# Score matmuls issued in turn for the two halves of the rows, and the norms' reciprocal roots as a power on GpSimd

## The chip, the cores and the metric

The kernel runs on one core of a Trainium2 chip. The core has a matmul engine (TensorE, PE in the profile, with its weight loads shown as PEld), VectorE (DVE), ScalarE (ACT), GpSimd (POOL) and a queue that issues transfers (SyncE, SP). The metric is device time in microseconds from the first to the last instruction of one execution; lower is better.

## The reference, cut to what matters

256 rows of width 1024 go through two layers of a first block and two layers of a second block, all in float32. What bears on the change:

```python
def rms_norm(x, g):
    y = x * lax.rsqrt(jnp.mean(x * x, axis=-1, keepdims=True) + EPS)
    return y * g

# first block, for each 128-row half t of the rows, 16 heads of 64:
logits = einsum("bqhd,bsd->bqhs", iqb, ik)            # 8 index heads of 64
score  = einsum("bqh,bqhs->bqs", iwb, relu(logits)) * IDX_SCALE
# the 64 best keys of each row are kept; the rest is masked
s = einsum("bqhd,bqkhd->bhqk", qb, kg) * scale
p = softmax(where(valid, s, -inf))
# second block: 8 heads of 96 the same way without selection, and a gated
# linear attention over chunks of 64:
a_intra = where(causal, einsum('bhncd,bhnsd->bhncs', q_t, k_t), 0.0)
```

Every `rms_norm` needs one reciprocal root for each row and normed group: of the whole row (ahead of each projection), of each head (q and k), of each of four groups of the state-space output, and of the latent vectors of the second block.

## The kernel before, in words

The work is one long program of projections. Activations lie transposed (features on partitions), 256 rows wide. Each weight slab of 128 by 1024 floats is loaded by SyncE into `raw` (line 443), copied to a high part by ScalarE (`whi`, line 446), and the rest is made by VectorE (`wlo`, line 447); 639 such slabs stream through five `raw` buffers. `lin_t` (lines 482 to 484) and `add_n` (499 to 501) then make three reduced-precision matmuls in place of each full one. Matmuls between activations (scores, transposes, sums) are made in float32, and each of them shows as two matmul instructions in the trace.

PSUM has four `pmm` tiles for projections and four `px` tiles for all else: scores, transposes (672), the sums of squares of a norm (554), the spreading of its root (575), and the modulation columns (`ada_part`, 697 to 702).

The order on each engine is not the written one. Every instruction has a priority by its place in the program (weight loads and splits have a raised one), and a planner that simulates the timeline picks, for each engine, the ready instruction of the best priority. Each engine then works its list strictly in order. Side work (attention, the linear attention, preparations) is written as Python generators that the projection loops advance step by step, so that its instructions fall between projections.

`rsqrt(v, n)` (lines 534 to 544) makes the root of n columns: a shifted bit pattern as first guess (538, 539) and three Newton steps of three operations (541 to 543), eleven VectorE instructions in a chain. It is called 28 times: 8 times by `Norm.close` for whole rows (n = 2), 8 times by `ssm_norm` (n = 2), 4 times for the heads of the first block (n = 32), 4 times for those of the second (n = 16), twice for the latents (n = 4) and twice in `gla` (n = 8). The value `v` comes from `mean_eps` (548). For n = 2 two matmuls against the identity (575) turn the root into a row that is copied (632) or used from PSUM.

Score matmuls of 64 features read rows 0 to 63 or rows 64 to 127 of the array, by the parity of the head. Before, `attention` issues for each 128-row half t two tiles: heads h0 and h0+2 (one parity), then h0+1 and h0+3 (the other), with a yield of the generator between them. `index_scores` issues for e = 0 and then e = 1 a tile of two heads each, and `gla` writes tile q = 0 and then q = 1 of a pair j.

Of the kernel before, what the change touches and what calls it, by code (L numbers as in the profile page):

```python
# [19 lines left out]
F32 = mybir.dt.float32  # L20
F32R = mybir.dt.float32r
I32 = mybir.dt.int32
AF = mybir.ActivationFunctionType
OP = mybir.AluOpType
AX = mybir.AxisListType

EPS = 1e-6
RSQRT_BITS = 0x5F3759DF
T = 256
D = 1024  # L30
NEG = -3.0e38
# [302 lines left out]
def program(ctx: ExitStack, tc: tile.TileContext, a, out, pp_at, cst_at):  # L334
    nc = tc.nc
    V, S, G, PE, SY = nc.vector, nc.scalar, nc.gpsimd, nc.tensor, nc.sync

    cpool = ctx.enter_context(tc.tile_pool(name="cpool", bufs=1))
# [43 lines left out]
        S.dma_start(pp[0], a["pp"][:, :PP0])  # L382
    V.memset(ones, 1.0)
    V.memset(eps, EPS)
    V.memset(hpi, math.pi / 2)

    def C(key):
        o, n = cst_at[key]
        return cst[1][:, o - 128:o - 128 + n] if o else cst[0]
# [18 lines left out]
    def t512(name="t512", dt=F32):  # L408
        return tmp.tile([128, 512], dt, name=name, tag="t512", bufs=N512)
# [4 lines left out]
    def tiny(n, name="tiny"):  # L414
        return tmp.tile([128, n], F32, name=name, tag=f"tiny{n}", bufs={24: 1, 16: 4, 64: 1}.get(n, 8))

    def pmm():
        return ps_mm.tile([128, 512], F32, name="pmm", tag="pmm", bufs=4)

    def px():  # L420
        return ps_x.tile([128, 512], F32, name="px", tag="px", bufs=4)
# [96 lines left out]
    def new_hl(n, name):  # L518
        k = (n + 3) // 4
        return HL([slot(F32R, name + "h") for _ in range(k)], [slot(F32R, name + "l") for _ in range(k)])  # L520

    def to_hl(dst, k, src, bias=None, scale=None, eng=None):

        if bias is not None:
            S.activation(dst.hi(k), src, AF.Identity, bias=bias)
            V.scalar_tensor_tensor(dst.lo(k), src, bias, dst.hi(k), OP.add, OP.subtract)  # L526
        elif scale is not None:
            S.activation(dst.hi(k), src, AF.Copy, scale=scale)
            V.scalar_tensor_tensor(dst.lo(k), src, scale, dst.hi(k), OP.mult, OP.subtract)
        else:  # L530
            S.activation(dst.hi(k), src, AF.Copy)
            (eng or V).tensor_tensor(dst.lo(k), src, dst.hi(k), OP.subtract)  # L532

    def rsqrt(v, n):

        q, r = tiny(n, "rq"), tiny(n, "rr")
        ri = r.bitcast(I32)
        V.tensor_scalar(ri, v.bitcast(I32), 1, None, OP.logical_shift_right)
        V.tensor_scalar(ri, ri, -1, RSQRT_BITS, OP.mult, OP.add)
        for _ in range(3):  # L540
            V.tensor_tensor(q, r, r, OP.mult)
            V.scalar_tensor_tensor(q, q, -0.5, v, OP.mult, OP.mult)
            V.scalar_tensor_tensor(r, q, 1.5, r, OP.add, OP.mult)
        return r

    def mean_eps(ss, n, width, eps_=EPS):
        v = tiny(n, "rv")
        V.tensor_scalar(v, ss, 1.0 / width, eps_, OP.mult, OP.add)
        return v
# [221 lines left out]
    def attention(heads, qT, kT, scale, bias, vN, out_hl):  # L771

        for h0 in heads:
            pr = {}
            for t, hs in ((1, (h0, h0 + 2)), (1, (h0 + 1, h0 + 3)), (0, (h0, h0 + 2)), (0, (h0 + 1, h0 + 3))):
                nk, nh = 128 * (t + 1), 2
                ps = px()[:, :2 * nk]
                for j, h in enumerate(hs):
                    PE.matmul(ps[:, j * nk:(j + 1) * nk], qT(h)[:, t * 128:(t + 1) * 128], kT(h)[:, :nk],  # L779
                              start=True, stop=True)  # L780
                s = t512("sc") if t else tmp.tile([128, 256], F32, name="sc", tag="sc", bufs=NSC)
                s = s.rearrange("p (h k) -> p h k", h=nh)
                V.scalar_tensor_tensor(s, ps.rearrange("p (h k) -> p h k", h=nh), scale,
                                       bias(t)[:, None, :].to_broadcast([128, nh, nk]), OP.mult, OP.add)
                m = tiny(4, "m")
                V.tensor_reduce(m[:, :nh], s, AX.X, OP.max, negate=True)
                z = tiny(4, "z")
                for j in range(nh):
                    S.activation(s[:, j, :], s[:, j, :], AF.Exp, bias=m[:, j:j + 1], accum_out=z[:, j:j + 1])
                V.reciprocal(z[:, :nh], z[:, :nh])  # L790
                for j, h in enumerate(hs):
                    V.tensor_scalar(s[:, j, :], s[:, j, :], z[:, j:j + 1], 0.0, OP.mult, OP.add)
                    pr[h, t] = s[:, j, :]
                yield
            for hp in range(h0, h0 + 4, 2):
                pt = {}
                for h in (hp, hp + 1):
                    ps = px()
                    PE.transpose(ps[:, 0:128], pr[h, 0], ident)
                    PE.transpose(ps[:, 128:256], pr[h, 1][:, 0:128], ident)  # L800
                    PE.transpose(ps[:, 256:384], pr[h, 1][:, 128:256], ident)
                    pt[h] = t512("pt")
                    S.activation(pt[h][:, :384], ps[:, :384], AF.Copy)
                po = px()
                for h in (hp, hp + 1):
                    e = (h % 2) * 64
                    PE.matmul(po[e:e + 64, :256], vN(0, h), pt[h][:, :256],  # L807
                              start=True, stop=False, skip_group_check=True)
                for h in (hp, hp + 1):
                    e = (h % 2) * 64  # L810
                    PE.matmul(po[e:e + 64, 128:256], vN(1, h), pt[h][:, 256:384],
                              start=False, stop=True, skip_group_check=True)
                to_hl(out_hl, hp // 2, po[:, :256])
                yield
# [8 lines left out]
    def block1(l):  # L823
# [6 lines left out]
        h = new_hl(8, "h")  # L830
# [19 lines left out]
        ps, pn = px(), [[pmm(), pmm()] for _ in range(2)]  # L850
# [49 lines left out]
        def index_scores(t, iqT, ikT):  # L900
            nk = 128 * (t + 1)
            iws = tiny(8, "iws")
            V.tensor_scalar(iws, mN[:, t, 96:104], IDX_SCALE, None, OP.mult)
            cz = C("caus")[:, 256 - nk:]
            sc = tmp.tile([128, nk], F32, name="bias", tag=f"bias{t}", bufs=1)
            for j in range(0, 4, 2):
                for e in range(2):
                    pl = px()
                    for i in range(2):
                        PE.matmul(pl[:, i * nk:(i + 1) * nk], iqT[64 * e:64 * e + 64, j + i, t * 128:(t + 1) * 128],  # L910
                                  ikT[64 * e:64 * e + 64, :nk], start=True, stop=True)
                    rl = t512("rl")
                    S.activation(rl[:, :2 * nk], pl[:, :2 * nk], AF.Relu)
                    for i in range(2):
                        V.scalar_tensor_tensor(sc, rl[:, i * nk:(i + 1) * nk],
                                               iws[:, 2 * (j + i) + e:2 * (j + i) + e + 1],
                                               cz if j + e + i == 0 else sc, OP.mult, OP.add)
            yield
            for r in range(8):
                m8 = tiny(8, "m8")  # L920
                V.max(m8, sc)
                V.match_replace(sc, m8, sc, SENT)
            V.tensor_scalar(sc, sc, SPLIT_AT, NEG, OP.is_gt, OP.mult)
            V.tensor_tensor(sc, sc, cz, OP.min)
            bias[t] = sc
# [46 lines left out]
        qT = lambda hh: TT["q"][hh // 8][64 * (hh % 2):64 * (hh % 2) + 64, (hh // 2) % 4, :]  # L972
        kT = lambda hh: TT["k"][hh // 8][64 * (hh % 2):64 * (hh % 2) + 64, (hh // 2) % 4, :]
# [29 lines left out]
        for g in range(4):  # L1003
            bc = {}
            for i, nm in enumerate("bc"):
                ps = lin_t("w_in", h, range(8))
# [20 lines left out]
        for n in range(16):  # L1027
            for _ in range(24 * (n + LAG) // 16 - 24 * (n + LAG - 1) // 16 if n + LAG else 0):
                next(att, None)
            g, j = divmod(n, 4)  # L1030
            if j == 0:
                ys[g] = slot(name="xs")
            ps = lin_t("w_in", h, range(8))
# [106 lines left out]
        for j in range(8):  # L1140
            ps = lin_t("w_out", mx, range(8))
# [38 lines left out]
        for j in range(8):  # L1180
            ps = lin_t("w_down", f, range(22))
# [490 lines left out]
    def gla(l, ef, gqf, gkf, ke, gvN, gr, ob):  # L1672
# [5 lines left out]
                         [ke[:, j * 256 + t * 128:j * 256 + (t + 1) * 128] for j in range(2)], 128, 128)  # L1678
        pms = [px(), px()]
        for j in range(2):  # L1680
            for q in range(2):
                for t in range(2):
                    c0 = j * 256 + t * 128
                    PE.matmul(pms[q][:, c0:c0 + 128], gkf[64 * q:64 * q + 64, c0:c0 + 128],
                              gqf[64 * q:64 * q + 64, c0:c0 + 128], start=True, stop=True)
# [6 lines left out]
        for n in range(3):  # L1692
            for hh in range(4):
                j, q = hh // 2, hh % 2
# [7 lines left out]
        for hh in range(4):  # L1702
            j, q = hh // 2, hh % 2
# [11 lines left out]
        pss, oos = px(), []  # L1715
# [19 lines left out]
        r = rsqrt(mean_eps(pss[:, :8], 8, 128), 8)  # L1735
# [43 lines left out]
```

## Time and profile before

| | us |
|---|---|
| median of 3 runs | 2309.45 |
| all runs | 2316.24, 2309.45, 2309.44 |
| profiled execution | 2316.91 |
| its span in the trace | 2315.1 |

The profiled execution is one more run with the profiler on; its span is the time from its first to its last instruction, and 1.8 us lie around it. It stands with the slowest of the three runs. Times in the rows are microseconds from the start of the span. A matmul's end is modelled in the trace, so a run of matmuls is best timed from its first start to the start of what follows.

### The profile page before, as it was taken

To read this page: it belongs to the slowest core of one execution; us is meant where nothing else is said; L and a number is where in the kernel's file an instruction comes from. 1 tells how busy PE (TensorE), PEld (TensorE's weight loads), DVE (VectorE), ACT (ScalarE), POOL (GpSimd) and SP (SyncE) were. 2 spreads that over 40 slices of the span, in tenths; PEclk is the share of its full clock that TensorE was granted. 3 is DMA by queue.
4 is the path that set the end of the run, shared out by engine and by line. 5 is a ranking of instruction groups with operands and counts; after the bars stand their busy time and mean duration, and the time that the engine had idled before them with its cause. 6 is when DMAs were issued, how large, how long until landed. Compare 5 with 4: busy or idle time off the path is not lost.

```text
span 2315.1 us, 46342 instructions
## 1 busy us (share of the span) xinstructions
PE 2214.8 (96%) x18142; PEld 2077.9 (90%) x18142; DVE 1745.4 (75%) x3612; ACT 1319.7 (57%) x2462; POOL 64.8 (3%) x94
## 2 busy tenths in 40 slices
PE   7999899999999999899989999989999999899999
PEld 5888798898998878888989998889999998899999
DVE  4688778669877689878689786867785578678853
ACT  4555666457656555665467655656565455555643
POOL 0000001000000000012000000000000000000000
PEclk9999999999999999999999998999999999999999
DMA  8665344665676664344655574734555546345553
GB/s 296 214 228 199 132 146 156 225 213 193 220 241 216 221 219 155 126 152 154 225 170 189 177 247 155 229 124 151 179 178 183 184 165 217 116 150 180 184 184 125
DMA packets 143466, 429.22 MB, mean 185 GB/s; under 512 B 34864, under 2 KB 40976, under 8 KB 143248
## 3 DMA queue, kind: packets, MB, share of 16 engines
q1 hardware_dynamic: 136496, 422.24, 55.4%
q10 hardware_dynamic: 6752, 4.02, 0.5%
q8 instruction: 143, 2.34, 0.4%
q14 instruction: 75, 0.61, 0.1%
HBM read 413.98 MB, written 12.22 MB: 184 GB/s over the span
## 4 chain that ended last, share of the span: by engine, by line
PE 88%; DVE 7%; DMA 3%; ACT 2%; issue 1%; SPq 0%; ACTq 0%; DVEq 0%
PE pmm L482 22%; PE pmm L483 22%; PE pmm L484 22%; PE pmm L499 3%; PE pmm L500 3%; PE pmm L501 3%; PE px L697 2%; DVE wlo L447 2%; DMA raw<-in_w 1%; PE px L779 1%; PE px L807 1%; PE px L1103 1%; ACT whi L446 1%; PE px L672 1%; DMA raw<-in_ada 1%
## 5 line engine op out<-in xcount | busy, mean ns | idle before, releaser
L446 ACT ACTIVATE whi<-raw 128x1024 fp32r<-128x1024 f32 x639 | 674.8, 1059 | 615.4 <-PE pmm L483 402.8
L447 DVE TENSOR_TENSOR wlo<-raw,whi 128x1024 fp32r<-128x1024 f32 x639 | 783.3, 1227 | 318.6 <-PE pmm L484 218.8
L482 PE MATMUL pmm<-hh,whi 128*128 128x256 f32 x2464 | 712.0, 290 | 38.2 <-DVE xs L980 11.4
L484 PE MATMUL pmm<-hh,wlo 128*128 128x256 f32 x2464 | 708.9, 289 | 2.4 <-DVE wlo L447 2.4
L483 PE MATMUL pmm<-hl,whi 128*128 128x256 f32 x2464 | 710.2, 289 | 0.7 <-DVE hl L526 0.4
L482 PEld LDWEIGHTS pmm<-hh,whi 128*128 128x128 f32 x2464 | 482.4, 196 | 47.1 <-issue 11.3
L484 PEld LDWEIGHTS pmm<-hh,wlo 128*128 128x128 f32 x2464 | 482.1, 196 | 6.2 <-issue 2.9
L483 PEld LDWEIGHTS pmm<-hl,whi 128*128 128x128 f32 x2464 | 482.7, 196 | 4.8 <-issue 2.1
L482 PE MATMUL pmm<-fh,whi 128*128 128x256 f32 x864 | 244.9, 284 | 0.0
L483 PE MATMUL pmm<-fl,whi 128*128 128x256 f32 x864 | 244.5, 283 | 0.0
L484 PE MATMUL pmm<-fh,wlo 128*128 128x256 f32 x864 | 244.3, 284 | 0.0
L482 PEld LDWEIGHTS pmm<-fh,whi 128*128 128x128 f32 x864 | 165.7, 192 | 0.5
L483 PEld LDWEIGHTS pmm<-fl,whi 128*128 128x128 f32 x864 | 165.7, 192 | 0.2
L484 PEld LDWEIGHTS pmm<-fh,wlo 128*128 128x128 f32 x864 | 165.5, 192 | 0.5 <-issue 0.2
L500 PE MATMUL pmm<-wlo,hh 128*128 128x512 f32 x256 | 103.5, 404 | 0.0
L499 PE MATMUL pmm<-whi,hh 128*128 128x512 f32 x256 | 100.7, 406 | 0.0
L501 PE MATMUL pmm<-whi,hl 128*128 128x512 f32 x256 | 100.3, 400 | 0.0
L483 PE MATMUL pmm<-yl,whi 128*128 128x256 f32 x256 | 73.0, 288 | 1.1 <-DVE yl L532 1.0
L484 PE MATMUL pmm<-yh,wlo 128*128 128x256 f32 x256 | 72.2, 287 | 0.3 <-DVE wlo L447 0.3
L482 PE MATMUL pmm<-yh,whi 128*128 128x256 f32 x256 | 72.1, 286 | 0.0
L697 PE MATMUL px<-raw,cwide 128*32 128x128 f32 x1536 | 66.5, 287 | 4.3 <-DMA raw<-in_ada 4.0
L697 PEld LDWEIGHTS px<-raw,cwide 128*32 128x32 f32 x1536 | 41.8, 112 | 19.3 <-issue 11.1
(553 smaller groups left out, 4247.6 us busy)
## 6 DMA issues: line engine op xcount, KB each, us to landing
raw<-in_w SPq DMA_DIRECT2D x639, 512.0 KB, 3.7
raw<-in_ada SPq DMA_DIRECT2D x96, 512.0 KB, 4.3
csb<-csd SPq DMA_DIRECT2D x16, 512.0 KB, 5.8
phd<-phases SPq DMA_DIRECT2D x8, 512.0 KB, 3.6
phasel<-phd SPq DMA_DIRECT2D x8, 512.0 KB, 4.4
dpd<-dp SPq DMA_DIRECT2D x4, 512.0 KB, 3.5
gl<-gd SPq DMA_DIRECT2D x32, 64.0 KB, 3.5
bl<-in_s5b SPq DMA_DIRECT2D x4, 512.0 KB, 5.5
```

The lines of the kernel that those rows point to most:

```text
L446: S.activation(hi, raw, AF.Copy)
L447: V.tensor_tensor(lo, raw, hi, OP.subtract)
L482: PE.matmul(ps[:m, :n], wh, src.hi(kt), start=q == 0, stop=False)
L483: PE.matmul(ps[:m, :n], wh, src.lo(kt), start=False, stop=False)
L484: PE.matmul(ps[:m, :n], wl, src.hi(kt), start=False, stop=q == len(kts) - 1)
L499: PE.matmul(ps[t][:, :n], src.hi(kt)[:, ts], w[0], start=start, stop=False)
L500: PE.matmul(ps[t][:, :n], src.hi(kt)[:, ts], w[1], start=False, stop=False)
L501: PE.matmul(ps[t][:, :n], src.lo(kt)[:, ts], w[0], start=False, stop=stop)
L672: PE.transpose(ps[:m, j * ncol:(j + 1) * ncol], s, ident[:ncol, :ncol])
L697: PE.matmul(pa[32 * j:32 * j + 32, :128], cwide[:, i, :], w[:, i * 128:(i + 1) * 128], start=i < 4, stop=i >= 4, skip_group_check=True)
L779: PE.matmul(ps[:, j * nk:(j + 1) * nk], qT(h)[:, t * 128:(t + 1) * 128], kT(h)[:, :nk], start=True, stop=True)
L807: PE.matmul(po[e:e + 64, :256], vN(0, h), pt[h][:, :256], start=True, stop=False, skip_group_check=True)
```

## The change

The eleven instructions of `rsqrt` become one: GpSimd raises `v` to the power of a column that holds -0.5. The column is set once at the start by VectorE. The score matmuls are issued head by head in turn for the two parities, into two PSUM tiles that are taken together; in `attention` this moves the second tile's matmuls ahead of the first tile's softmax and of the yield behind it. Nothing else is changed.

```diff
+    mhalf = cpool.tile([128, 1], F32, name="mhalf")
+    V.memset(mhalf, -0.5)
...
     def rsqrt(v, n):
-        q, r = tiny(n, "rq"), tiny(n, "rr")
-        ri = r.bitcast(I32)
-        V.tensor_scalar(ri, v.bitcast(I32), 1, None, OP.logical_shift_right)
-        V.tensor_scalar(ri, ri, -1, RSQRT_BITS, OP.mult, OP.add)
-        for _ in range(3):
-            V.tensor_tensor(q, r, r, OP.mult)
-            V.scalar_tensor_tensor(q, q, -0.5, v, OP.mult, OP.mult)
-            V.scalar_tensor_tensor(r, q, 1.5, r, OP.add, OP.mult)
+        r = tiny(n, "rr")
+        G.tensor_tensor(r, v, mhalf.to_broadcast([128, n]), OP.pow)
         return r
...
             for t, hs in ((1, (h0, h0 + 2)), (1, (h0 + 1, h0 + 3)), (0, (h0, h0 + 2)), (0, (h0 + 1, h0 + 3))):
                 nk, nh = 128 * (t + 1), 2
-                ps = px()[:, :2 * nk]
-                for j, h in enumerate(hs):
-                    PE.matmul(ps[:, j * nk:(j + 1) * nk], qT(h)[:, t * 128:(t + 1) * 128], kT(h)[:, :nk],
-                              start=True, stop=True)
+
+                if hs[0] == h0:
+                    pss = [px()[:, :2 * nk] for _ in range(2)]
+                    for h in range(h0, h0 + 4):
+                        j = (h - h0) // 2
+                        PE.matmul(pss[(h - h0) % 2][:, j * nk:(j + 1) * nk], qT(h)[:, t * 128:(t + 1) * 128],
+                                  kT(h)[:, :nk], start=True, stop=True)
+                ps = pss[hs[0] - h0]
...
             for j in range(0, 4, 2):
+                pls = [px(), px()]
+                for i in range(2):
+                    for e in range(2):
+                        PE.matmul(pls[e][:, i * nk:(i + 1) * nk],
+                                  iqT[64 * e:64 * e + 64, j + i, t * 128:(t + 1) * 128],
+                                  ikT[64 * e:64 * e + 64, :nk], start=True, stop=True)
                 for e in range(2):
-                    pl = px()
-                    for i in range(2):
-                        PE.matmul(pl[:, i * nk:(i + 1) * nk], iqT[64 * e:64 * e + 64, j + i, t * 128:(t + 1) * 128],
-                                  ikT[64 * e:64 * e + 64, :nk], start=True, stop=True)
                     rl = t512("rl")
-                    S.activation(rl[:, :2 * nk], pl[:, :2 * nk], AF.Relu)
+                    S.activation(rl[:, :2 * nk], pls[e][:, :2 * nk], AF.Relu)
...
         for j in range(2):
-            for q in range(2):
-                for t in range(2):
+            for t in range(2):
+                for q in range(2):
                     c0 = j * 256 + t * 128
                     PE.matmul(pms[q][:, c0:c0 + 128], gkf[64 * q:64 * q + 64, c0:c0 + 128],
                               gqf[64 * q:64 * q + 64, c0:c0 + 128], start=True, stop=True)
```

## Rows read from the trace of the kernel before

**Rows 1.** Page, the chain that ended last, by engine.
```profile
PE 88%; DVE 7%; DMA 3%; ACT 2%; issue 1%; SPq 0%; ACTq 0%; DVEq 0%
```

**Rows 2.** Timeline of PE, index scores (910), first layer: start, length, instruction, count.
```profile
134.98 1.14 PE L910 MATMUL px<-ikT,iqT 64*128 64x256 f32 x8
136.05 0.50 PE L499 MATMUL pmm<-whi,hh 128*128 128x512 f32 x1
...
136.71 1.13 PE L910 MATMUL px<-ikT,iqT 64*128 64x256 f32 x4
137.77 0.50 PE L501 MATMUL pmm<-whi,hl 128*128 128x512 f32 x1
...
152.62 1.26 PE L910 MATMUL px<-ikT,iqT 64*128 64x128 f32 x16
153.81 0.50 PE L499 MATMUL pmm<-whi,hh 128*128 128x512 f32 x1
```

**Rows 3.** Timeline of PE, attention scores (779), 128 keys, in both layers.
```profile
219.91 0.71 PE L779 MATMUL px<-kT,qT 64*128 64x128 f32 x4
220.55 0.39 PE L482 MATMUL pmm<-hh,whi 128*128 128x256 f32 x1
...
950.96 0.72 PE L779 MATMUL px<-kT,qT 64*128 64x128 f32 x8
951.61 0.39 PE L484 MATMUL pmm<-hh,wlo 128*128 128x256 f32 x1
```

**Rows 4.** Timeline of PE, scores of the linear attention (1684).
```profile
1508.99 1.71 PE L1684 MATMUL px<-gqk 64*128 64x128 f32 x16
1510.63 0.55 PE L1697 MATMUL px<-gv,kN 64*64 64x128 f32 x6
```

**Rows 5.** All that touches the root: min/median/max ns; last line, who waited for 543.
```profile
L541 DVE TENSOR_TENSOR rq<-rr x84: 146/161/198, 11.5 to 2134.6; 128x2 f32<-128x2 f32 x48, 128x32 f32<-128x32 f32 x12, 128x16 f32<-128x16 f32 x12, 128x4 f32<-128x4 f32 x6
...
  PE px L575: 6.4, 4
```

**Rows 6.** Timeline of the first norm, at the start.
```profile
10.87 0.17 DVE L548 TENSOR_SCALAR rv<-xss 128x2 f32<-128x2 f32 x1
...
14.51 0.16 DVE L543 SCALAR_TENSOR_TENSOR rr<-rq,rr 128x2 f32<-128x2 f32 x1
14.82 1.19 PE L575 MATMUL px<-cst,rr 128*128 128x128 f32 x4 [6.04 <-ACT whi L446]
...
15.94 3.66 PE L697 MATMUL px<-raw,cwide 128*32 128x128 f32 x64
```

**Rows 7.** Windows: busy us of engines (instructions), granted PE clock, DMA share, GB/s.
```profile
16.00:18.00 2.00, 2.00 (x41) 1.96 (x44) 1.90 (x6) 0.41 (x2) 0.00 (x0) 1.00 0.01 4
...
510.00:542.00 32.00, 26.40 (x211) 24.95 (x210) 30.82 (x72) 21.82 (x43) 0.00 (x0) 0.96 0.57 181
...
1468.00:1473.00 5.00, 1.79 (x13) 1.59 (x12) 4.90 (x22) 4.73 (x14) 0.00 (x0) 0.85 0.65 215
```

**Rows 8.** Timeline of the linear attention's norm, second block, first layer.
```profile
1529.06 0.17 DVE L548 TENSOR_SCALAR rv<-px 128x8 f32<-128x8 f32 x1 [1.90 <-PE px L554]
...
1529.70 1.23 DVE L447 TENSOR_TENSOR wlo<-raw,whi 128x1024 fp32r<-128x1024 f32 x1
...
1532.66 1.60 PE L575 MATMUL px<-cst,rr 128*128 128x128 f32 x12 [1.63 <-DVE rr L543]
```

**Rows 9.** GpSimd's operations by line: count, ns min/median/max.
```profile
L565 POOL TENSOR_TENSOR sq<-sq x24: 724/1208/2657, 326.9 to 1096.8; 128x256 f32<-128x256 f32 x24
...
L751 POOL TENSOR_TENSOR tb2q<-cst,rows x8: 249/830/5201, 845.7 to 1508.4; 128x32 f32<-128x32 f32 x8
```

**Rows 10.** Timeline of VectorE, the stretch of GpSimd's longest operation.
```profile
1502.42 1.22 DVE L447 TENSOR_TENSOR wlo<-raw,whi 128x1024 fp32r<-128x1024 f32 x1
...
1507.31 0.56 DVE L1580 TENSOR_TENSOR mq<-mq,rr 128x384 f32<-128x384 f32 x1
```

**Rows 11.** Timeline of PE, the stall behind the second head group's scores.
```profile
243.50 0.55 PE L482 MATMUL pmm<-hh,whi 128*128 128x256 f32 x1 [2.87 <-DVE xs L980]
```

More of the change, by code (lines that the diff above doesn't have):

```diff
@@ L27 @@
 EPS = 1e-6
-RSQRT_BITS = 0x5F3759DF
 T = 256
```

## The prediction

> **What bounds the kernel now.** I read the chain of work that ended last first, then the timeline of PE where scores are made, then everything that touches the root, the busy time by stretches, and GpSimd's own operations. The chain lies on PE for 88% of the span and on DVE for 7% [rows 1]. So a matmul saved is saved time nearly everywhere, and a DVE instruction saved counts only where PE waits for DVE. The reader should look in each view for one thing: does what follows start later because of the work that the change touches?
>
> **Scores in turn.** The trace of before already shows what turning is worth, because the planner has mixed the two parities in places. Eight score instructions of 256 keys that alternate between the row halves occupy 134.98 to 136.05, 1.07 us. Four of one parity occupy 136.71 to 137.77, 1.06 us [rows 2]. At 128 keys four of one parity take 0.64 us and eight in turn 0.65 us [rows 3]. A run that finds a partner is therefore free. Sixteen at 128 keys take 1.19 us where most alternate [rows 2], and 1.64 us in the linear attention, where the written order puts two of one parity together [rows 4].
>
> The sites: attention in the first block has 16 pairs of runs (two layers, four head groups, two halves). Read in the timeline, three are in turn already and nine could each save about one run of 0.64 us or the like, 5.8 us in all. Four of these nine stand right ahead of a stall like the one of 2.87 us in which PE waits for a convolution on DVE [rows 11]; PE would reach that stall sooner and wait longer, so I count five, 3.2 us. The index scores of the later half have two unpaired runs of 1.06 us in each layer, one of which becomes free: 2.1 us. The linear attention saves 1.64 less 1.19, 0.45 us, in each of two layers: 0.9 us. The second block's heads use 96 rows, which overlap both halves, so nothing alternates there: zero. That is 6.2 us; I take 6. The bounds are zero, if PE gets only to waits for DVE, and 9, if all of it counts.
>
> The move costs little. The second tile is taken before the first softmax rather than after it, out of four `px` tiles that transposes, spread roots and the modulation columns also use. What it can hold back is one such user for the time of a score run, 1.06 us at most [rows 2]; I take zero, since the planner chooses by readiness and PE has projections in `pmm` to go on with. No transfer moves in the program. The first tile's softmax starts two instructions later, 0.5 us by the same row, and PE doesn't wait for it there.
>
> **The power.** Removed are 28 calls of eleven DVE instructions. One takes 0.16 us, the median of 84 such steps [rows 5], so a call frees 1.8 us of DVE and all 28 free 49 us. As a chain it is longer: from the start of the mean to the spread 3.60 us passed in the linear attention, with one weight split of 1.23 us among it [rows 8]; less the split that is 2.4 us for twelve links, 0.2 us each.
>
> What is added is one GpSimd instruction in each call. No row shows a power. The nearest below is a two-input product of 32 columns, 0.25 us at its fastest. Above, the same row's slowest, 5.2 us [rows 9], is the longest GpSimd time in this trace; it is made of waiting, but a power worked in many steps could come to as much. I take 1.0 us for 2 to 8 columns: nearer the product, since 2 columns are few, and about four products' worth of work. The heads' calls with 16 and 32 columns may take a few times that; their roots are used several operations later, by the product behind the rotation, and PE has projections meanwhile. GpSimd is idle before nearly every call; the memset of -0.5 is one small DVE instruction at the start. The new wait is on GpSimd for the mean and on PE for GpSimd, two handovers of about 0.1 us, in place of none on DVE and one on PE.
>
> Where it comes back:
> At the start, the mean begins at 10.87, the root ends at 14.67, the spread starts at 14.82, and only then the 64 modulation matmuls at 15.94, which free the weight buffers [rows 6]. With a power the root is there at about 10.87 + 0.17 + 0.1 + 1.0, 12.1 us: 2.5 us sooner. The transfers stand still in 16 to 18, a DMA share of 0.01 [rows 7], so loading starts again earlier by that: I take 2, bounds 0 and 2.5.
> PE waits directly for the last Newton step at four calls, 6.4 us in total [rows 5]. The power has 3.5 us in each before it is later than now, by the 3.60 us above; I take 5 of the 6.4, leaving one split of 1.23 us to stand in the way once. Bounds 0 and 6.4.
> DVE is nearly full where the first block's second norm ends (30.82 of 32 us, PE busy 26.40) and before the linear attention's inputs (4.90 of 5, PE 1.79) [rows 7]. Each has its like in the other layer, so 1.8 us could be freed four times, 7.2 us. But ACT makes the high parts that these splits need, and the planner fills DVE with other ready work: I take 3. Bounds 0 and 7.2. The other calls are covered by PE's projections: zero, and at most one split of 1.23 us each if that cover is short.
>
> **The sum.** 6 + 2 + 5 + 3 is 16 us. The profiled execution took 2316.9 us, so it would take 2300.9. It stands 7.5 us above the median of the runs shown, 2309.45; from the median I forecast 2293.5, say 2294 us. A measurement of this kernel tells about 0.3%, 7 us, from no change.
>
> **A lock between DVE and GpSimd.** The slowest GpSimd product, with its 249 ns of work, took 5.2 us, while DVE ran two-input operations one behind the other, from a split that starts at 1502.42 to a product that ends at 1507.87 [rows 9, 10]. A power issued into such a stretch would wait for its end. The Trainium skill, SBUF — State Buffer, on the ports that VectorE and GpSimd share, states that whichever of a two-SBUF-input VectorE operation and a GpSimd operation starts first holds the pair for its whole length and the other is fully blocked; the trace agrees for GpSimd as the loser (5.2 us). By that rule the power is late just where weight splits crowd, and a long power would also stop the splits.
>
> **Rivals.**
> The power waits behind the splits. Until now the Newton steps and the splits share DVE in turn; without the steps, splits stand back to back and each holds GpSimd off. For it: 639 splits of 1.23 us, and the median of the 32-column product is 830 ns against 249 at best [rows 9]. Against it: the splits themselves wait for ACT and for buffers. With two splits, 2.5 us, in the way at each call the four direct waits give 2 instead of 5, the start gives 1, the full stretches of DVE give 1, and with 6 from the scores that is 10: 2300 us. The rule of the Trainium skill cited above, SBUF — State Buffer, would make it so.
> Hidden anyway. PE reaches the next wait for DVE, ACT or a slab sooner, and the scores' and the roots' gains are given back; the planner makes another order from other costs. For it: PE's stalls behind DVE are of 2.87 us, longer than any one gain here [rows 11]. Against it: 88% of the chain on PE [rows 1]. A quarter of the 16 us is left, or none: 2305 to 2309, say 2306.
> Slower: the power is long and holds DVE. It decides from about 3.5 us for a call, where the power ends later than the Newton chain does now [rows 8]. At 5.2 us the start and the four direct waits turn from a gain of 7 into a loss of 1.7 times 5, 8.5; in the four full DVE stretches 5.2 less the 1.8 freed is 3.4 us, 14 in all, in place of 3 gained. With 6 from the scores that is 16.5 lost: 2326 us. The 32-column calls could add to it. For it: no row shows a power. Against it: two columns are little work.
> The turn isn't kept: the planner may issue the scores in another order than written, as it already mixed some. Then 6 falls away: 2300. I put it with the second rival and the forecast's upper part.
>
> **Chances and range.** Forecast 0.50, with its own range 2283 to 2302; behind the splits 0.15; hidden 0.19; slow power 0.16. Faster by over 0.3% (below 2302.5) are nearly all of the first, most of the second and a little of the third: 0.63. Slower (above 2316.4) is the last: 0.15. The rest, 0.22, is no change. The range runs from 2280, with all of 9 + 2.5 + 6.4 + 7.2 and some 4 us of PE time now lost at the lower clock behind stalls (the granted clock is 0.85 on the mean of 1468 to 1473, so part of it lies at 1.2 GHz and not 2.4, where PE was busy for only 1.79 of 5 us [rows 7]), to 2313, which takes in the hidden case and leaves out most of the slow one.
>
> **What would show it.** Scores right: every run of 8 score instructions of the first block takes about 1.07 or 0.65 us, and no run of four stands alone. Power right: GpSimd's new row at about 1 us for 2 columns; the spread at the start near 12.3; no wait of PE for the root left at the four calls; DVE's busy time down by some 49 us. Wrong: a GpSimd median above 3.5 us, DVE splits with longer times beside a power, or PE's stalls behind the convolutions grown by what the scores saved.

## The result, and the profile after

The changed kernel takes 2284.0 us in the median of five runs (2277.9 to 2286.1); the kernel before, run beside it five times, takes 2310.4. The ratio is 0.9876, with a 95% interval of 0.9864 to 0.9889: 28.7 us less by the ratio, 26.4 by the medians. The profiled execution took 2286.07 us, with a span of 2283.3, 31.8 less than the span before.

The page of the changed kernel, busy time by engine and the chain by engine [rows 1]:

```profile
PE 2199.2 (96%) x18142; PEld 2064.5 (90%) x18142; DVE 1703.0 (75%) x3305; ACT 1321.0 (58%) x2462; POOL 126.7 (6%) x122
...
PE 87%; DVE 6%; issue 3%; DMA 2%; ACT 2%; POOL 1%; SPq 0%; ACTq 0%; DVEq 0%; POOLq 0%
```

PE issues the same 18142 matmuls and is busy 2199.2 us, against 2214.8 before: 15.6 of the 31.8 us are busy time and 16.2 are idle time. (Ends of matmuls are modelled, so short waits can stand in the busy time.) The mean granted clock of these two executions is 0.980 against 0.981, so the clock gave nothing here. DVE is relieved of 42.4 us and 307 instructions.

GpSimd's operations by line and shape; busy us and mean ns stand behind the bar [rows 9]:

```profile
L538 POOL TENSOR_TENSOR rr<-rv,mhalf 128x16 f32<-128x16 f32 x4 | 23.4, 5852 | 85.8 <-DVE rv L543 85.8
L538 POOL TENSOR_TENSOR rr<-rv,mhalf 128x32 f32<-128x32 f32 x4 | 21.9, 5475 | 145.9 <-DVE rv L543 145.9
L538 POOL TENSOR_TENSOR rr<-rv,mhalf 128x2 f32<-128x2 f32 x16 | 13.7, 856 | 980.3 <-DVE rv L543 980.3
```

The prices are the line to read first: 0.86 us on the mean for 2 columns, where I had guessed 1.0, but 5.9 and 5.5 us on the mean for 16 and 32.

At the start [rows 6], timeline of the changed kernel:

```profile
11.57 0.70 POOL L538 TENSOR_TENSOR rr<-rv,mhalf 128x2 f32<-128x2 f32 x1 [11.13 <-DVE rv L543]
...
12.32 1.22 PE L570 MATMUL px<-cst,rr 128*128 128x128 f32 x4 [3.32 <-POOL rr L538]
...
13.47 2.50 PE L692 MATMUL px<-raw,cwide 128*32 128x128 f32 x48
```

The spread starts at 12.32 in place of 14.82 and the modulation matmuls at 13.47 in place of 15.94. Among PE's waits, that for the root is now this one alone [rows 5]:

```profile
PE px L570 <- POOL rr L538: 3.3, 1, 3.3
```

The scores on PE, index scores and attention of the first layer and the linear attention [rows 2 to 4]:

```profile
131.77 1.14 PE L909 MATMUL px<-ikT,iqT 64*128 64x256 f32 x8
132.83 0.50 PE L500 MATMUL pmm<-whi,hh 128*128 128x512 f32 x1
...
133.50 1.13 PE L909 MATMUL px<-ikT,iqT 64*128 64x256 f32 x4
134.56 0.50 PE L502 MATMUL pmm<-whi,hl 128*128 128x512 f32 x1
...
213.20 0.72 PE L777 MATMUL px<-kT,qT 64*128 64x128 f32 x8
213.86 0.39 PE L485 MATMUL pmm<-hh,wlo 128*128 128x256 f32 x1
...
1481.86 1.71 PE L1685 MATMUL px<-gqk 64*128 64x128 f32 x16
1483.49 0.65 PE L1698 MATMUL px<-gv,kN 64*64 64x128 f32 x8
```

These lines show that little happened: attention's eight in turn are there, as some were before, but there are still eight index scores together and then four alone for 1.06 us, and sixteen scores of the linear attention in 1.63 us where before they took 1.64. Counted over all score matmuls of these three places (each from its start to the start of the next matmul, at most 0.33 us), PE spent 33.3 us on them before and 31.3 after. The stall behind the second head group's scores [rows 11] is still there:

```profile
237.41 0.55 PE L483 MATMUL pmm<-hh,whi 128*128 128x256 f32 x1 [2.97 <-DVE xs L981]
```

Windows of the changed kernel over the like of the two stretches in which DVE was nearly full [rows 7]:

```profile
492.60:524.60 32.00, 27.17 (x229) 26.35 (x228) 30.00 (x61) 22.57 (x44) 1.06 (x2) 0.94 0.53 176
1440.00:1445.00 5.00, 1.09 (x4) 0.64 (x4) 5.00 (x16) 0.89 (x4) 0.00 (x0) 0.72 0.66 199
```

DVE is still nearly full there (30.00 of 32, 5.00 of 5) and PE hardly better off (27.17 after 26.40, and 1.09 after 1.79): the freed time was filled with other work.

### The profile page after: what moved, and what is told of

Same layout as the page of the kernel before. It is cut to its first block, busy times and chain, and to the rows that moved or that the text cites. A ratio compares the mean times of both kernels' runs of the same rounds, so it can differ in the third digit from the quotient of the medians.

```text
span 2283.3 us, 46079 instructions
## 1 busy us (share of the span) xinstructions
PE 2199.2 (96%) x18142; PEld 2064.5 (90%) x18142; DVE 1703.0 (75%) x3305; ACT 1321.0 (58%) x2462; POOL 126.7 (6%) x122
## 4 chain that ended last, share of the span: by engine, by line
PE 87%; DVE 6%; issue 3%; DMA 2%; ACT 2%; POOL 1%; SPq 0%; ACTq 0%; DVEq 0%; POOLq 0%
PE pmm L483 22%; PE pmm L485 22%; PE pmm L484 22%; PE pmm L500 3%; PE pmm L501 3%; PE pmm L502 3%; PE px L692 2%; DVE wlo L448 2%; PE px L806 1%; DMA raw<-in_ada 1%; PE px L777 1%; PE px L1104 1%; DMA raw<-in_w 1%; PE px L667 1%; DVE xs L981 1%
## 5 line engine op out<-in xcount | busy, mean ns | idle before, releaser
L538 POOL TENSOR_TENSOR rr<-rv,mhalf 128x2 f32<-128x2 f32 (+3 forms) x26 | 62.3, 2396 | 1284.5 <-DVE rv L543 1284.5
L483 PE MATMUL pmm<-yh,whi 128*128 128x256 f32 x256 | 73.3, 287 | 0.0
```

Source lines behind the costliest of these rows:

```text
L483: PE.matmul(ps[:m, :n], wh, src.hi(kt), start=q == 0, stop=False)
L538: G.tensor_tensor(r, v, mhalf.to_broadcast([128, n]), OP.pow)
```

## The experiments

Theory at first: both parts pay, and one term of the sum is too small. The minus side of a diff is the changed kernel in the first four runs, the kernel before in the three that give the power to some calls alone (`rpow` is the changed kernel's `rsqrt`), and the kernel named in the rest. The eleven Newton instructions are left out where they come back, and `...` marks other lines left out. Each run was timed beside the kernel before; its ratio is to that one, and 0.001 of it is 2.3 us.

**The scores alone.** The eleven Newton instructions stay on DVE:

```diff
-        r = tiny(n, "rr")
-        G.tensor_tensor(r, v, mhalf.to_broadcast([128, n]), OP.pow)
+        q, r = tiny(n, "rq"), tiny(n, "rr")
...
```

> The scores' turn alone; the root by Newton steps on DVE as before. By the prediction's sum the scores are worth 6 us (bounds 0 to 9): about 2304 us beside 2310, ratio 0.997. If the scores are the term that was mis-sized, nearly all of the gain of 26 us stands here: 2290 or less. If the turn isn't kept or is given back at the next wait: 2308 to 2312.

Measured: 2315.7, ratio 1.0011 (1.0000 to 1.0022). No gain. The second layer's index scores, timeline of PE in this kernel:

```profile
831.86 1.14 PE L914 MATMUL px<-ikT,iqT 64*128 64x256 f32 x8
832.93 0.50 PE L500 MATMUL pmm<-wlo,hh 128*128 128x512 f32 x1
...
834.05 1.13 PE L914 MATMUL px<-ikT,iqT 64*128 64x256 f32 x4
835.11 0.50 PE L501 MATMUL pmm<-whi,hl 128*128 128x512 f32 x1
...
836.01 1.13 PE L914 MATMUL px<-ikT,iqT 64*128 64x256 f32 x4
837.07 0.39 PE L483 MATMUL pmm<-hl,whi 128*128 128x256 f32 x1
```

Two runs of four stand alone at 256 keys, and four more such runs of four follow at 128 keys. The program writes every four in turn; the planner, which takes the ready instruction of the best priority, has sorted them its own way. Counted as above, all scores together take 34.1 us of PE here, 0.8 more than before. The rival that the turn isn't kept holds.

**The power alone.** Scores in the order of before, in all three places.

```diff
-                    PE.matmul(pss[(h - h0) % 2][:, j * nk:(j + 1) * nk], qT(h)[:, t * 128:(t + 1) * 128],
-                              kT(h)[:, :nk], start=True, stop=True)
...
+                    PE.matmul(ps[:, j * nk:(j + 1) * nk], qT(h)[:, t * 128:(t + 1) * 128], kT(h)[:, :nk],
+                              start=True, stop=True)
...
```

> The power alone, everywhere; the scores as before. By the prediction's sum it is worth 10 us (start 2, four direct waits 5, full DVE stretches 3): about 2300 us, ratio 0.9957. If the root is the term that was mis-sized, since the state-space norms which I costed at nothing pay too: about 2290 us (20 us, what is left of 26 when the scores keep their 6), ratio 0.991. If the two parts need one another, the gains of the two kernels don't add up to 26.

Measured: 2278.5, ratio 0.9843 (0.9830 to 0.9856): 36 us, more than the whole change brings. So the root is the mis-sized term, and the turn takes something back.

**Newton steps for the wide calls.**

```diff
+        if n <= 8:
             r = tiny(n, "rr")
             G.tensor_tensor(r, v, mhalf.to_broadcast([128, n]), OP.pow)
             return r
+        q, r = tiny(n, "rq"), tiny(n, "rr")
...
```

> The changed kernel, but with a power only for 2, 4 and 8 columns and the Newton steps for the heads' calls of 16 and 32 columns. The trace after the change shows those powers at about 5.5 us each and PE waiting for them, 3 to 4 us at a time, ahead of the heads' transposes. If these stalls cost PE time: about 8 us less than the changed kernel, 2276. If they only take the place of stalls that DVE would cause there with its Newton steps: no difference, 2284. Slower than 2284 if DVE's relief in the linear attention's heads is worth more than the stalls.

Measured: 2276.9, ratio 0.9834 (0.9821 to 0.9846), below the changed kernel's interval. In the changed kernel PE waits ahead of the heads' transposes for the product with the 16-column root, 2.98 us in this line of its timeline:

```profile
1442.62 1.09 PE L667 MATMUL px<-cst,mq 128*96 128x128 f32 x4 [2.98 <-DVE mq L1581]
```

From the spread of the latents' root to the first scores of the linear attention the first layer takes 92.6 us with these powers, 88.2 without and 88.4 before.

**Both the power and the Newton steps.** The steps' result is used by nothing.

```diff
+        q, r = tiny(n, "rq"), tiny(n, "rr2")
...
         r = tiny(n, "rr")
         G.tensor_tensor(r, v, mhalf.to_broadcast([128, n]), OP.pow)
```

> The changed kernel, with the eleven DVE instructions of the Newton root issued as well, their result used by nothing. If the shorter way from the sums to the spread is what pays: within 5 us of the changed kernel, about 2287. If DVE's relief is what pays (42 us less of DVE's busy time): the power's gain is lost and only the scores' stays, about 2303. If half and half: 2295.

Measured: 2280.2, ratio 0.9842 (0.9828 to 0.9857); DVE is busy 1743.4 us, as before the change. So the gain isn't DVE's relief. What is left is that the root is there sooner; a run below tests that from the other side, with the relief and without the early root. The kernel is even faster than the changed one, with more work. The planner makes another list for each program, and some us come and go with the list (13 between two kernels at the end); the smaller differences below are to be read with that.

**Where the root was late.** The state-space norm shows it. VectorE of the kernel before, a part of its timeline from the mean (548) to the last Newton step (543):

```profile
340.97 0.16 DVE L548 TENSOR_SCALAR rv<-px 128x2 f32<-128x2 f32 x1 [0.33 <-PE px L554]
...
342.66 0.16 DVE L538 TENSOR_SCALAR rr<-rv 128x2 int32<-128x2 int32 x1
...
343.20 1.22 DVE L447 TENSOR_TENSOR wlo<-raw,whi 128x1024 fp32r<-128x1024 f32 x1
...
344.67 0.16 DVE L539 TENSOR_SCALAR rr<-rr 128x2 int32<-128x2 int32 x1
...
346.43 1.02 DVE L1099 TENSOR_TENSOR dd<-dd,cbm 128x384 f32<-128x384 f32 x2
347.37 0.15 DVE L541 TENSOR_TENSOR rq<-rr 128x2 f32<-128x2 f32 x1
347.44 1.22 DVE L447 TENSOR_TENSOR wlo<-raw,whi 128x1024 fp32r<-128x1024 f32 x1
...
361.77 0.16 DVE L543 SCALAR_TENSOR_TENSOR rr<-rq,rr 128x2 f32<-128x2 f32 x1
```

The twelve links take some 0.16 us each, but among them stand splits and products of the scan: 20.96 us from the start of the mean to the end of the root. The same call in the changed kernel takes 1.19 us:

```profile
328.63 0.16 DVE L543 TENSOR_SCALAR rv<-px 128x2 f32<-128x2 f32 x1 [0.33 <-PE px L549]
...
328.87 0.95 POOL L538 TENSOR_TENSOR rr<-rv,mhalf 128x2 f32<-128x2 f32 x1 [3.54 <-DVE rv L543]
```

The four calls of this norm in the first layer took 20.96, 22.18, 12.73 and 4.53 us before and take 0.95 to 1.19 after. In the second layer they took 20.96, 22.19, 13.04 and 4.53; three of them now take 0.93 to 1.06, and one takes 4.63, because GpSimd was still at five memsets of its own when the mean came, and a split followed.

**The state-space norm alone** has the power, eight calls; all else as before.

```diff
-            r = rsqrt(mean_eps(sumsq([xs[:, j, :] for j in range(4)], pairs=SQ_PAIRS[g]), 2, 512, 16 * EPS), 2)
+            r = rpow(mean_eps(sumsq([xs[:, j, :] for j in range(4)], pairs=SQ_PAIRS[g]), 2, 512, 16 * EPS), 2)
```

> The power in the eight calls of the state-space norm alone; everything else as before. My prediction costed these calls at nothing, covered by PE's projections: then 2310 to 2314. By the stage times of the four kernels with the power, the two state-space stages are 8.5 and 9.5 us shorter: then 18 us, 2296.

Measured: 2299.8, ratio 0.9949 (0.9937 to 0.9962): 11.8 us. That is less than the stage times said, but far from nothing. Those times were taken from kernels with all small powers, and they run up to the spread of the next norm, whose own way was 2.8 and 3.0 us shorter there (6.04 and 6.15 us before, 3.22 and 3.19 after): 18 less 5.8 is 12.2. In this kernel's own trace the two stages are 7.8 and 6.4 us shorter.

**The blocks' norms alone**, the other eight calls of 2 columns.

```diff
-            S.activation(self.r, spread(rsqrt(self.v, 2), px()), AF.Copy)
+            S.activation(self.r, spread(rpow(self.v, 2), px()), AF.Copy)
```

> The power in the eight calls of the blocks' norms alone, scores as before, Newton steps elsewhere. By my sum these bring the start's 2, the full DVE stretches' 3 and a part of the four direct waits, some 7 us: 2304. By the stage times of the kernel with all small powers they bring the larger part of what the state-space norms (11.5 us) leave of 42: 20 to 28 us, 2284 to 2291.

Measured: 2285.4, ratio 0.9887 (0.9870 to 0.9903): 26 us from eight instructions. Their ways show a sum of that size. From the start of the mean to the first matmul of the spread the eight calls took 3.95, 6.04, 7.28, 6.15, 8.90, 5.08, 7.51 and 5.89 us in the kernel before, 50.8 in all; here they take 1.00 to 3.29, 22.6 in all, 28.2 less. The longest, mean, root and spread in the kernel before:

```profile
1391.59 0.16 DVE L548 TENSOR_SCALAR rv<-px 128x2 f32<-128x2 f32 x1 [1.22 <-PE px L554]
...
1398.35 0.15 DVE L543 SCALAR_TENSOR_TENSOR rr<-rq,rr 128x2 f32<-128x2 f32 x1
...
1400.49 0.60 PE L575 MATMUL px<-cst,rr 128*128 128x128 f32 x4
```

Four splits stand among its links. The same call here:

```profile
1369.71 0.16 DVE L556 TENSOR_SCALAR rv<-px 128x2 f32<-128x2 f32 x1 [1.34 <-PE px L562]
...
1369.95 0.69 POOL L551 TENSOR_TENSOR rr<-rv,mhalf 128x2 f32<-128x2 f32 x1 [207.37 <-DVE rv L556]
...
1372.00 0.60 PE L583 MATMUL px<-cst,rr 128*128 128x128 f32 x4
```

That 28 lies near 26 isn't a proof, since PE has projections during a part of each way: its idle time in the 20 us behind each mean falls from 13.7 to 4.6 us in all, and the rest shows only later in the stages.

**All calls of 2 to 8 columns, no turn.**

```diff
+        if n <= 8 and not newton:
+            return rpow(v, n)
         q, r = tiny(n, "rq"), tiny(n, "rr")
```

> Power for 2 to 8 columns, Newton steps for 16 and 32, all scores in the order of before. By the two earlier runs: the power alone 2278, less the 3 to 4 us that PE waits for the 16 columns in each of two layers: 2271. Against the run with the turn in the index scores and the linear attention it says what those two are worth: 3 us by my sum, 0 if it is given back at the next wait.

Measured: 2269.4, ratio 0.9819 (0.9806 to 0.9833): 41.8 us, the best kernel here. (`newton` is never set.) State-space norm 11.8, blocks' norms 26.1: 3.9 us are left for the four calls of 4 and 8 columns, which no run has alone; the norm of the linear attention, which holds two of them, is 1.7 and 2.5 us shorter in the two layers. A part of the gain is clock: the granted clock is 0.984 to 0.986 in this kernel's runs and 0.979 to 0.983 in those of the kernel before beside it, on the mean 0.005 higher. Of some 2200 us of PE's work that is 11 us, an estimate from these numbers. Its page, busy time and the chain:

```profile
PE 2195.9 (97%) x18142; PEld 2065.2 (91%) x18142; DVE 1716.1 (76%) x3394; ACT 1320.6 (58%) x2462; POOL 78.9 (3%) x114
...
PE 90%; DVE 5%; ACT 2%; issue 1%; DMA 1%; ACTq 0%; POOL 0%; SPq 0%; DVEq 0%
```

**The same with late powers**, against the run before. Three powers of exponent 1 ahead of each.

```diff
-SLOW = 0
+SLOW = 3
...
         for _ in range(SLOW):
             w = tiny(n, "rw")
             G.tensor_tensor(w, v, mone.to_broadcast([128, n]), OP.pow)
             v = w
         r = tiny(n, "rr")
```

> The kernel of the next run with three more powers, of exponent 1, ahead of each power of 2 to 8 columns, one behind the other: the root of 2 columns comes 2.1 to 2.6 us later, at 2.8 to 3.5 us, about where the Newton chain ends now. DVE is relieved as before. If the shorter way alone pays, as the kernel with both the power and the Newton steps says, nearly all of the gain is gone: 2300 to 2312. If the relief of DVE or the new order of work pays: 2272 to 2285. Over 2316 if a long GpSimd operation also holds DVE, my slow rival.

Measured: 2306.1, ratio 0.9979 (0.9969 to 0.9989): 4.9 of the 41.8 us are left. From the mean to the root the calls of 2 columns now take 3.3 to 5.1 us, but for one of 8.0, and those of 8 columns 7.0. PE waits for them:

```profile
PEld px L592 <- POOL rr L560: 9.3, 3, 5.8
PE px L592 <- POOL rr L560: 8.5, 3, 5.4
PE px L592 <- POOL vb L1424: 10.2, 2, 5.1
```

The last line is the two calls of 8 columns: the wait is put down to a small memset that GpSimd works right behind the last power. DVE is relieved (1714.7 us busy against 1716.1) and its splits keep their length (1.22 us on the mean in both kernels), so it is the late root that costs, and not a long GpSimd operation that holds DVE.

The state-space stages keep their gain (223.5 us from the last attention score to the second norm in the first layer, 229.9 before), since 4 us is still less than 21. The eight ways of the blocks' norms are back at 41.2 us in all. The linear attention, where the Newton root took 3.54, loses: from its first score to the first score behind its norm it takes 30.7 us, against 25.6 before.

**Which turn costs.** In the first four kernels with the turn attention's scores of the second layer took 68.5 to 73.3 us from first to last; in the kernel before and with the power alone they took 64.1. My theory blamed attention's own turn; it was undone in the kernel with Newton steps for the wide calls.

```diff
-                if hs[0] == h0:
-                    pss = [px()[:, :2 * nk] for _ in range(2)]
...
+                ps = px()[:, :2 * nk]
...
```

> Power for 2 to 8 columns, Newton steps for 16 and 32, the turn in the index scores and in the linear attention, but attention's scores in the order of before. All four kernels with attention's turn took 68.5 to 73.3 us from the first to the last score of the first block's second layer, the two without it 64.1. If the turn itself does that: 4 to 9 us less than the kernel that differs in this alone (2277), so 2268 to 2273. If the planner would have found some other order with the same stalls: no difference, 2277.

Measured: 2278.2, ratio 0.9857 (0.9842 to 0.9872), and the stretch still takes 72.7 us. The theory fell. What was left was the index scores' turn, undone in the same kernel, with attention's turn kept:

```diff
             for j in range(0, 4, 2):
-                pls = [px(), px()]
-                for i in range(2):
-                    for e in range(2):
+                for e in range(2):
+                    pl = px()
+                    for i in range(2):
...
```

> Power for 2 to 8 columns, the turn in attention and in the linear attention, the index scores in the order of before. My last theory, that attention's turn costs 4 to 9 us in the second layer, fell: the kernel without it has the same 72.7 us there. What all kernels with 68 to 73 us there share is the turn of the index scores. If the index scores' turn alone costs: this run takes 2264 to 2269, as fast as the kernel with no turn (2269.4) or by up to 5 us faster, with about 64 us in that stretch. If any turn costs: 2273 to 2279.

Measured: 2271.8, ratio 0.9824 (0.9807 to 0.9841); the stretch takes 64.1 us. Against the kernel without any turn (0.9819), attention's and the linear attention's turns cost and bring nothing that can be measured. (Beside turned index scores attention's turn went with 5 us less by the ratios, 1.3 by the medians, with intervals that just overlap.) Up to here the index scores' turn goes with the longer stretch in every kernel that has it. VectorE of the changed kernel there, and PE's weight load for the transposes, a part of the timeline:

```profile
892.52 0.29 DVE L925 TENSOR_TENSOR bias<-bias,cst 128x128 f32<-128x128 f32 x1
...
895.46 0.75 DVE L782 SCALAR_TENSOR_TENSOR sc<-px,bias 128x256 f32<-128x256 f32 x2
...
898.08 0.18 PEld L798 LDWEIGHTS px<-cst,sc 128*128 128x128 f32 x1 [4.07 <-issue]
```

The early half's mask, which is made of the index scores and keeps the best keys of each row, gets its last step at 892.52, 12.4 us after the first attention score; only then can its softmaxes begin, and PE stands idle for four us ahead of the transposes. Without any turn and with the small powers it starts 8.0 us ahead of that score.

**The mask made early.** Small powers, only the index scores turned, and one empty step of the side work is left out; the run after it is its control, without a turn.

```diff
                     turn()
                     yield
-                    yield
+                    if nm == "k":
+                        yield
                     if nm == "q":
```

> Power for 2 to 8 columns, the index scores turned and nothing else; beside that one empty step of the side work is left out, so that the early half's mask, made of the index scores by eight rounds of maxima on DVE, stands on DVE's queue ahead of attention's softmaxes (before weight split 231 of the program, not 238). Theory: the index scores' turn costs because the planner then puts these rounds behind the splits of the attention stage; the mask ends 12 to 14 us after attention's first score, and the softmaxes and the transposes wait for it. Then with the mask early the stall of 4 us ahead of the transposes is gone, the stretch takes about 64 us, and the kernel 2266 to 2271. If the turn costs in another way (px tiles held, ACT): 2275 to 2280.

> The kernel of the run before without any turn: only the empty step left out, power for 2 to 8 columns. It says what the step alone does: by the theory the mask was in time already (8 us ahead of attention), so no difference to 2269.4, 2267 to 2272; and the run before should be within 3 us of this one.

Measured: 2277.2 with the turn (0.9849, 0.9834 to 0.9864), 2283.4 without (0.9875, 0.9858 to 0.9892). The mask's last step now starts 14.7 us ahead of attention's first score, and the stretch takes 62.9 us, as the theory has it. But the control, with that step 12.5 us ahead, takes 68.4 there with stalls at other places, so the mask alone doesn't decide, and what makes the stretch long stays open. Between the second layer's index scores and its attention PE has a long wait in both kernels; timeline of PE in the turned one:

```profile
856.02 0.58 PE L487 MATMUL pmm<-hh,whi 128*128 128x256 f32 x1 [6.24 <-DVE cvb L1000]
```

The control has 6.28 us there. But the kernel with neither the turn nor the missing step waits 4.06 us at the same place and 1.76 twelve us later, so this explains little of why the totals miss both expectations. Both kernels are 4 to 5 us behind it already at the 65th weight split, in the first layer; where the rest lies stays open. Here the turned kernel is 6 us the faster. And the one missing step alone made 13 us (0.9875 against 0.9819): so much can hang on the list that the planner makes. Against that the 41.8 us and the 26 stand clear, while the 3 to 8 us of the turn and the 5.5 of the wide powers do not. The 11.8 of the state-space norm rests on its stage times beside the total. Whether turned index scores cost or pay is a matter of the list around them.

## Why the prediction came out as it did

**The number and the direction** were right: 2294 forecast, 2284 measured, within 2280 to 2313. That the number came so near is luck: the sum has 6 us for the scores and 10 for the power, where the power alone brought 36 and the turn on top of it took 7.6.

**Scores, 6 us: wrong.** The step that failed is taking the written order as the issued one; the description of the kernel and the prediction both say that a planner orders the work, and the rival that the turn isn't kept had only a share of the chances. PE's time for scores fell by 2.0 us, in the linear attention by none, and alone the turn brought nothing. In three pairs of kernels that differ in the turn it went with 2.5 (Newton roots), 7.6 (all powers) and 3.5 us (small powers) more, though the first interval touches no change and the last two overlap; in the fourth, with the mask early, with 6 less.

**Start, 2 us: right at the spread.** It came at 12.32, forecast near 12.3; no row separates what it brought to the end.

**Direct waits, 5 of 6.4 us: right as far as it goes.** Of the waits for the root only the start's is left; the norm of the linear attention is 1.7 and 2.5 us shorter in the two layers.

**The other calls, zero, and full DVE stretches, 3 us: the term that was mis-sized.** I measured the Newton chain where PE waits for it, 3.60 us [rows 8], and took that as its length everywhere, with PE's projections as cover. In the state-space stage it is 21 to 22 us for two calls of each layer, because DVE's list puts a split or a product between the links; the cover wasn't as long as that. There I had zero and 11.8 us were measured. For the blocks' norms the sum has at most 2 for the start, 3 for the full stretches and a part of the direct waits; 26 were measured. Yet the trace of the kernel before had them: these eight ways take 50.8 us there, not eight times 3.60, which is 28.8. That it is the earlier root and not DVE's free time, the runs with both and with late powers show, for all small powers together; how the 26 us fall upon single stalls stays open.

**Heads' calls, zero: wrong, small.** They take 2.9 to 9.2 us each, and PE waits about 3 us in each layer of the second block. Between the two kernels without a turn the wide powers cost 5.5 us (0.9843 against 0.9819; the intervals overlap only at their ends), between the two with it 9.7 (0.9876 against 0.9834).

**Slow rival: its threshold was nearly right.** With roots at 3.3 to 5 us in place of 1, nearly all of the gain is gone; but 4.9 us are left, not a loss, since the state-space norm still gains.

Read from kernel to kernel, the small powers bring 41.8 us, the wide ones take 5.5 and the turn 7.6, which leaves the measured 28.7. These are steps of one chain of kernels, so that they add up shows nothing; by other pairs the wide powers cost 9.7 and the turn 3.5.

## What to carry to other kernels

Measure a dependent chain where it stands, from its first start to its last end, at every call: on an in-order engine with other work its length is its links plus all that stands between them, and one instruction on an idle engine can take the place of 21 us. Before counting on an order of instructions, look in the trace for whether the planner keeps it. A helper's price at its smallest size says nothing of its largest: split by size.

## What the runs showed of the hardware that was not expected

A power on GpSimd costs by the column: in the changed kernel at best 0.70 us for 2, 1.01 for 4, 1.64 for 8, 2.90 for 16 and 5.42 for 32, about 0.16 us for each column on top of 0.4.

The 16 columns took 2.90 us in two calls and 8.44 and 9.18 in the others. Timeline of GpSimd and VectorE in the slow one:

```profile
1426.36 8.44 POOL L538 TENSOR_TENSOR rr<-rv,mhalf 128x16 f32<-128x16 f32 x1 [34.45 <-DVE rv L543]
...
1427.40 1.22 DVE L448 TENSOR_TENSOR wlo<-raw,whi 128x1024 fp32r<-128x1024 f32 x1
...
1431.83 0.22 DVE L763 TENSOR_TENSOR mq<-ru,rv 128x64 f32<-128x64 f32 x1
...
1434.83 1.03 DVE L1581 TENSOR_TENSOR mq<-mq,rr 128x384 f32<-128x384 f32 x2 [2.79 <-POOL rr L538]
```

DVE worked, mostly two-input operations, one behind the other until 1432.05, and the power ended 2.75 us later, about what it takes undisturbed: GpSimd was held off, as the prediction's rows showed. The other direction, that a long power would stop the splits, is not seen. A power of 32 columns with a split inside it, from the timeline:

```profile
88.91 5.42 POOL L538 TENSOR_TENSOR rr<-rv,mhalf 128x32 f32<-128x32 f32 x1 [66.94 <-DVE rv L543]
...
90.06 1.22 DVE L448 TENSOR_TENSOR wlo<-raw,whi 128x1024 fp32r<-128x1024 f32 x1
```

The split takes its usual 1.22 us while the power is under way, and the power's 5.42 lies on the line of 0.16 us a column, so neither waited for the other. The Trainium skill, SBUF — State Buffer, on its two separate sides, says that of a VectorE operation with two SBUF inputs and a GpSimd operation whichever starts first holds the shared ports for its whole instruction; with GpSimd as the loser this trace agrees (8.44 us against 2.90), with GpSimd as the first it does not (a split of 1.22 us inside 88.91 to 94.33), as far as GpSimd's recorded spans can be trusted.
